# The norm's weights as one row, spread by a TensorE product, and the first tile scaled in halves

## The chip, the cores and the metric

The kernel runs on one core of a Trainium2 chip. The metric is the device time of one execution in microseconds (us); of the kernel before there are three timed runs and one profiled execution. TensorE is called PE, VectorE DVE, ScalarE ACT, GpSimd POOL, and SP is the engine that issues the DMAs.

## The reference

One decoder block on 1024 tokens of width 1024, float32. The part that matters here is the start:

```python
def rms_norm(x, g):
    xf = x.astype(jnp.float32)
    r = lax.rsqrt(jnp.mean(xf * xf, axis=-1, keepdims=True) + RMS_EPS)
    return (xf * r).astype(x.dtype) * g
...
        h = rms_norm(x, norm_g[layer])
        proj = h @ w_in[layer]
```

The projection is split into differential attention (q, k, v, z) and sparse attention (q, six kv parts, z, gates). Two of the kv parts are compressed: blocks of 32 tokens with a stride of 16 get a position term, go through a small two-layer network and give the compressed keys and values. Three sparse branches, the differential attention, two output gates, one output projection and the residual follow.

## The kernel before

Tokens are tiled by 128 (eight tiles). `load_x` brings one tile of x (512 KB) in, sums its squares on ACT (`xs`, `xss`), takes the power -0.5 on POOL (`xr`), multiplies by it and by the norm's weights on DVE (L235), transposes the tile on PE in two halves of four blocks (L152), and writes the transposed halves twice: rounded on ACT (`xh`, L240) and the remainder on DVE (`xl`, L241). The norm's weights lie in `ng_b`, 128 partitions times 1024, loaded by one DMA that reads the 4 KB row 128 times (L228).

`load_w` brings 512 or fewer columns of the projection in as eight tiles `raw` of 128 rows, splits each into a rounded part `whi` (ACT, L199) and a remainder `wlo` (POOL, L200); `raw` has four buffers. `mm_tokens` sums 24 products per token tile, three for each of eight k: whi by xh, wlo by xh, whi by xl (L208 to L210), in PSUM buffers that alternate between the kinds A and S.

The projection runs in chunks. The first (kv, 384 columns, `w_c0`) goes along with `load_x`; for each tile it copies the first two kv parts out (`kvraw`), transposes them, copies them (`kvt`, L263) and writes them to DRAM (`kv_d`, L264), and normalises a key head pair by `rms_heads`: square on ACT, sums `ss` on DVE, `r` on POOL (L135), the product `qn` on DVE (L143), a transpose on PE, then `kh` on ACT and `kl` on DVE. The second chunk (408 columns, `w_c1`) does the same with another key, and gates. The third (512 columns, nq) holds the compression: `cmp_flat` loads `kv_d` back as `kvT` (L317; one buffer, two loads per pass), adds the position term (`flat`, L320, DVE) and feeds the products at L332. There are eight `flat` steps.

The program's order on each engine isn't the order of the code: a scheduler builds it from its own timeline, and each engine then runs its list in order. SP issues all loads and stores on one queue; it has eight DMA semaphores that it uses in turn, so the ninth issue waits for the first to land.

Of the kernel before, what the change touches and what calls it, by code (L numbers as in the profile page):

```python
# [8 lines left out]
F32 = mybir.dt.float32  # L9
F32R = mybir.dt.float32r  # L10
AF = mybir.ActivationFunctionType
ALU = mybir.AluOpType
# [15 lines left out]
def block_kernel(ctx: ExitStack, tc: tile.TileContext, x, norm_g, w_in, dq_g, dk_g, lq1, lk1, lq2, lk2,  # L28
                 sub_g, nq_g, nk_g, cmp_pos, cmp_w1, cmp_b1, cmp_w2, w_out, out):
    nc = tc.nc  # L30
# [12 lines left out]
    def bcast(src, n):  # L43
        return bass.AP(tensor=src.tensor, offset=src.offset, ap=[[0, 128], [1, n]])

    def S_tile():
        return psS.tile([128, 1024], F32, tag="S", name="S")

    def T_tile():
        return psT.tile([128, 512], F32, tag="T", name="Tp")  # L50
# [97 lines left out]
    def transposed(src, nb):  # L148

        Tp = T_tile()  # L150
        for b in range(nb):
            nc.tensor.transpose(Tp[:, 128 * b:128 * b + 128], src[:, 128 * b:128 * b + 128], ident)  # L152
        return Tp[:, :nb * 128].rearrange("p (b t) -> p b t", t=128)
# [10 lines left out]
    with ExitStack() as p1:  # L164
# [16 lines left out]
        def load_w(wk, c0, c1, extra=None, perm=False, between={}):  # L181
            n = c1 - c0
            hi = wk.tile([128, 8, 512], F32R, tag="whi", name="whi")
            lo = wk.tile([128, 8, 512], F32R, tag="wlo", name="wlo")
            for k in range(8):
                for tt in between.get(k, ()):
                    load_x(between["xp"], tt)
                raw = wr.tile([128, 512], F32, tag="raw", name="raw")
                nc.sync.dma_start(raw[:, :n], w_in[128 * k:128 * k + 128, c0:c1])
                m = n  # L190
                if extra is not None:
                    m = n + extra[1] - extra[0]
                    nc.sync.dma_start(raw[:, n:m], w_in[128 * k:128 * k + 128, extra[0]:extra[1]])
                h_, l_, r_ = hi[:, k, :m], lo[:, k, :m], raw[:, :m]
                if perm:
                    h_ = h_.rearrange("p (g k d) -> p k g d", g=4, k=2)
                    l_ = l_.rearrange("p (g k d) -> p k g d", g=4, k=2)
                    r_ = r_.rearrange("p (k g d) -> p k g d", g=4, k=2)
                nc.scalar.activation(h_, r_, AF.Copy)  # L199
                nc.gpsimd.tensor_tensor(l_, r_, h_.bitcast(F32), op=ALU.subtract)  # L200
            return hi, lo
# [22 lines left out]
        def load_x(xp, tt):  # L224
            xt = xp.tile([128, T], F32, tag="xt", name="xt", bufs=5)
            nc.sync.dma_start(xt, x[128 * tt:128 * tt + 128])
            if tt == 0:
                nc.sync.dma_start(ng_b, bcast(norm_g, 1024))  # L228
            xs = xp.tile([128, T], F32, tag="xs", name="xs", bufs=1)
            ss = small.tile([128, 1], F32, tag="xss", name="xss")  # L230
            nc.scalar.activation(xs, xt, AF.Square, accum_out=ss)
            nc.vector.tensor_scalar(ss, ss, 1.0 / T, EPS, op0=ALU.mult, op1=ALU.add)
            r = small.tile([128, 1], F32, tag="xr", name="xr")
            nc.gpsimd.tensor_tensor(r, ss, neghalf[:, :1], op=ALU.pow)
            nc.vector.scalar_tensor_tensor(xt, xt, r, ng_b, op0=ALU.mult, op1=ALU.mult)  # L235
            t0 = 128 * tt
            for hf in range(2):
                X3 = transposed(xt[:, 512 * hf:512 * hf + 512], 4)
                k = slice(4 * hf, 4 * hf + 4)
                nc.scalar.activation(xh[:, k, t0:t0 + 128], X3, AF.Copy)  # L240
                nc.vector.tensor_tensor(xl[:, k, t0:t0 + 128], X3, xh[:, k, t0:t0 + 128].bitcast(F32), op=ALU.subtract)  # L241


        with ExitStack() as pc:
            xp = pc.enter_context(tc.tile_pool(name="xp", bufs=1))
            ng_b = xp.tile([128, 1024], F32, name="ng_b")
            load_x(xp, 0)
            w_c0 = load_w(wB, C_NKV, C_NKV + 384, between={"xp": xp, 3: (1,), 5: (2,), 7: (3,)})
            load_gains(1, nk_g, 3)
            for tt in range(NT):  # L250
                if tt + 4 < NT:
                    load_x(xp, tt + 4)
                if tt == 6:
                    load_consts(xp)
                t0 = 128 * tt
                if tt == 3:
                    w_c1 = load_w(wA, C_NKV + 384, C_NKV + 768, extra=(C_NG, C_NG + 24))
                A = mm_tokens(*w_c0, tt, 384)
                raw = st.tile([128, 512], F32, tag="qn", name="kvraw", bufs=3)
                nc.scalar.activation(raw[:, :256], A[:, :256], AF.Copy)  # L260
                kn = rms_heads(st, A[:, 256:384], 2, None)
                kvt = st.tile([128, 4, 128], F32, tag="z", name="kvt")[:, :2]
                nc.vector.tensor_copy(kvt, transposed(raw, 2))  # L263
                nc.sync.dma_start(kv_d[:, :, t0:t0 + 128].rearrange("b p t -> p b t"), kvt)  # L264
                k_pairs(kn, 1, G_KS, "nk", 0, tt)
# [435 lines left out]
    with ExitStack() as p3:  # L701
# [31 lines left out]
        for i, qt in enumerate(order):  # L733
# [7 lines left out]
            for h in range(4):  # L741
# [8 lines left out]
                                               op0=ALU.mult, op1=ALU.add)  # L750
# [17 lines left out]
            r = small.tile([128, 4], F32, tag="orr", name="orr")  # L768
# [30 lines left out]
```

## Time and profile before

| | us |
|---|---|
| three timed runs | 825.58, 829.02, 829.96 |
| median | 829.02 |
| profiled execution | 827.36 |
| its span, first to last instruction | 825.6 |
| PE busy | 777.7 (94%) |
| DVE, ACT, POOL busy | 515.8, 367.7, 358.5 |

The span is what the trace covers; the rest of the execution's time lies around it. PE's busy time counts pipelined products that overlap, so the distance from one product's start to the next says more than a product's own duration. A wait in brackets is the idle time of the engine before the instruction, with what ended it.

### The profile page before, as it was taken

Reading aid. Unit: us, or ns where it says so; the run is one execution under the profiler, and the core shown is the slowest. Engines: PE = TensorE matmul, PEld = TensorE weight load, DVE = VectorE, ACT = ScalarE, POOL = GpSimd, SP = SyncE. Lnnn points to the kernel's source line nnn. Section 1 sums busy time; section 2 is a strip of 40 time slices with the busy share of each in tenths; the row PEclk is TensorE's granted clock in tenths of the full one; section 3 lists DMA queues with packets and bytes.
Section 4 is the critical chain, followed back from the end, with each engine's and each line's share of the span. In section 5 each row is a group of like instructions: output and inputs, shape, how many; then the busy total and the mean of one; then the engine's idle time right before and its main releaser. Section 6 shows DMA issues by size and latency. Waiting matters only on the chain.

```text
span 825.6 us, 12841 instructions
## 1 busy us (share of the span) xinstructions
PE 777.7 (94%) x4457; PEld 643.0 (78%) x4457; DVE 515.8 (62%) x1183; ACT 367.7 (45%) x811; POOL 358.5 (43%) x385
## 2 busy tenths in 40 slices
PE   5999799999999999999899999999999798888997
PEld 4899788888888888888677788777777478687975
DVE  4654644368634338941698688785954296599843
ACT  6543131141323322121688656756564365477510
POOL 6834272250624525040487535354443135647421
PEclk9999899999999999999999999999999899999999
DMA  8637464151434423157643223130204504424133
GB/s 285 174 72 234 109 204 131 26 147 58 136 92 120 125 52 102 52 148 197 180 127 90 90 90 91 40 93 24 64 26 153 129 1 166 136 70 115 64 128 115
DMA packets 74257, 91.99 MB, mean 111 GB/s; under 512 B 13904, under 2 KB 48848, under 8 KB 74064
## 3 DMA queue, kind: packets, MB, share of 16 engines
q1 hardware_dynamic: 74192, 91.18, 38.3%
q8 instruction: 35, 0.57, 0.3%
q14 instruction: 30, 0.25, 0.1%
HBM read 63.89 MB, written 27.26 MB: 110 GB/s over the span
## 4 chain that ended last, share of the span: by engine, by line
PE 70%; DVE 11%; DMA 8%; POOL 4%; issue 3%; ACT 2%; SPq 2%; POOLq 0%; DVEq 0%; ACTq 0%
PE S L440 9%; PE A L632 6%; PE Tp L627 6%; PE S L210 5%; PE S L208 5%; PE S L209 5%; PE A L208 5%; PE A L210 5%; PE A L209 5%; PE A L480 3%; PE A L482 3%; PE A L481 3%; DVE P L444 2%; DMA raw<-in_w_in_dram 2%; PE Tp L152 2%
## 5 line engine op out<-in xcount | busy, mean ns | idle before, releaser
L446 ACT ACTIVATE P<-P,nm 128x128 f32<-128x128 f32 (+7 forms) x136 | 101.3, 749 | 35.8 <-DVE nm L444 26.3
L135 POOL TENSOR_TENSOR r<-ss,neghalf 128x8 f32<-128x8 f32 (+2 forms) x41 | 55.8, 1362 | 119.1 <-DVE ss L133 113.7
L200 POOL TENSOR_TENSOR wlo<-raw,whi 128x512 fp32r<-128x512 f32 (+2 forms) x64 | 82.5, 1314 | 51.4 <-ACT whi L199 51.4
L500 ACT ACTIVATE pT<-Tp 128x512 f32<-128x512 f32 (+3 forms) x118 | 66.2, 574 | 79.8 <-PE Tp L627 60.7
L208 PE MATMUL S<-whi,xh 128*128 128x512 f32 (+2 forms) x224 | 86.9, 388 | 1.2 <-ACT xh L240 0.7
L210 PE MATMUL S<-whi,xl 128*128 128x512 f32 (+2 forms) x224 | 87.1, 389 | 0.0
L208 PE MATMUL A<-whi,xh 128*128 128x512 f32 (+2 forms) x224 | 86.6, 387 | 0.0
L209 PE MATMUL S<-wlo,xh 128*128 128x512 f32 (+2 forms) x224 | 86.5, 386 | 0.0
L210 PE MATMUL A<-whi,xl 128*128 128x512 f32 (+2 forms) x224 | 86.0, 384 | 0.0
L209 PE MATMUL A<-wlo,xh 128*128 128x512 f32 (+2 forms) x224 | 85.9, 384 | 0.0
L596 POOL TENSOR_SCALAR P<-P,ssum 128x128 f32<-128x128 f32 (+7 forms) x72 | 52.9, 753 | 51.1 <-DVE ssum L592 31.8
L632 PE MATMUL A<-pT,vsw 128*64 128x256 f32 x528 | 67.3, 394 | 7.3 <-ACT pT L500 5.3
L440 PE MATMUL S<-nsaK,QH 128*128 128x384 f32 (+2 forms) x192 | 67.5, 360 | 2.0 <-DVE nm L444 1.8
L444 DVE CUSTOM_DVE_ANT_0 P<-S,D 128x128 f32<-128x128 f32 (+7 forms) x96 | 60.1, 660 | 14.5 <-PE S L440 8.3
L440 PE MATMUL S<-nsaK,QL 128*128 128x384 f32 (+2 forms) x192 | 60.7, 330 | 0.0
L632 PEld LDWEIGHTS A<-pT,vsw 128*64 128x64 f32 x528 | 35.2, 139 | 32.3 <-ACT pT L500 8.0
L596 POOL TENSOR_SCALAR Pw<-Pw,ssum 128x640 f32<-128x640 f32 (+3 forms) x56 | 40.7, 745 | 44.9 <-DVE ssum L592 37.5
L498 DVE COPY pT<-Tp 128x512 f32<-128x512 f32 (+3 forms) x62 | 38.5, 621 | 33.8 <-PE Tp L627 31.5
L415 POOL TENSOR_TENSOR QL<-q,QH 128x1024 fp32r<-128x1024 f32 x16 | 38.9, 2429 | 47.6 <-ACT QH L414 45.9
L160 DVE RECIPROCAL e<-e 128x512 f32<-128x512 f32 (+1 forms) x18 | 57.1, 3175 | 0.6
L199 ACT ACTIVATE whi<-raw 128x512 fp32r<-128x512 f32 (+2 forms) x64 | 36.5, 605 | 43.4 <-DMA raw<-in_w_in_dram 37.3
L480 PE MATMUL A<-woh,ch 128*128 128x512 f32 x128 | 51.9, 405 | 2.9 <-ACT ch L726 2.9
(186 smaller groups left out, 1820.5 us busy)
## 6 DMA issues: line engine op xcount, KB each, us to landing
raw<-in_w_in_dram SPq DMA_DIRECT2D x48, 256.0 KB, 3.1
xt<-in_x_dram SPq DMA_DIRECT2D x16, 512.0 KB, 3.8
w<-in_cmp_w_dram SPq DMA_DIRECT2D x16, 256.0 KB, 3.8
q<-nq_d SPq DMA_DIRECT2D x16, 256.0 KB, 4.2
xa_d<-xt SPq DMA_DIRECT2D x16, 256.0 KB, 2.0
q<-dq_d SPq DMA_DIRECT2D x16, 256.0 KB, 4.2
xt<-xa_d SPq DMA_DIRECT2D x8, 512.0 KB, 3.2
out_dram<-xt SPq DMA_DIRECT2D x16, 256.0 KB, 2.1
```

Of the source, the lines that this page charges most:

```text
L160: nc.vector.reciprocal(e, e)
L200: nc.gpsimd.tensor_tensor(l_, r_, h_.bitcast(F32), op=ALU.subtract)
L208: nc.tensor.matmul(A[:, :n], a, hi[:, k, :n], start=(k == 0), stop=False)
L209: nc.tensor.matmul(A[:, :n], a, lo[:, k, :n], start=False, stop=False)
L210: nc.tensor.matmul(A[:, :n], b, hi[:, k, :n], start=False, stop=(k == 7))
L440: nc.tensor.matmul(S[a][:, c0:c1], Q[:, heads[a]], Ks[a][:, w0 + c0 - o:w0 + c1 - o], start=Q is QH, stop=Q is QL)
L444: nc.vector.tensor_tensor_reduce(out=Ps[a][:, :n], in0=S[a][:, o:o + n], in1=biases[a], scale=-slopes[a], scalar=3e38, op0=ALU.add, op1=AL ...
L446: nc.scalar.activation(Ps[a][:, :n], Ps[a][:, :n], AF.Exp, scale=-1.0, bias=nm, accum_out=ssums[a])
L480: nc.tensor.matmul(A, ch[:, k], woh[:, k, c], start=(k == 0), stop=False)
L500: nc.scalar.activation(pT[:, :n], Tp[:, :n], AF.Copy)
L596: nc.gpsimd.tensor_scalar(P[:, :n], P[:, :n], ssum[:, g2, j:j + 1], 1.0, op0=ALU.mult, op1=ALU.mult)
L632: nc.tensor.matmul(O[64 * j:64 * j + 64, 256 * gp:256 * gp + 256], vsw[:, br, k0 + kt, 64 * j:64 * j + 64], pT[:, 256 * j:256 * j + 256], ...
```

## The change

The norm's weights are loaded as one row of 1024 on one partition. DVE fills a row of 128 ones. PE multiplies the ones by the row, half by half (fp32, one row deep), so each of the 128 output partitions gets the row; DVE copies both halves from PSUM to `ng_b`. For tile 0 only, the scaling at L235 is two instructions of 512 columns, each ahead of its half's transposes.

```diff
             if tt == 0:
-                nc.sync.dma_start(ng_b, bcast(norm_g, 1024))
+
+                g_row = xp.tile([1, 1024], F32, name="g_row")
+                nc.sync.dma_start(g_row, bass.AP(tensor=norm_g.tensor, offset=norm_g.offset, ap=[[1024, 1], [1, 1024]]))
+                ones = xp.tile([1, 128], F32, name="ones")
+                nc.vector.memset(ones, 1.0)
+                G = S_tile()
+                for hf in range(2):
+                    c = slice(512 * hf, 512 * hf + 512)
+                    nc.tensor.matmul(G[:, c], ones, g_row[:, c], start=True, stop=True)
+                    nc.vector.tensor_copy(ng_b[:, c], G[:, c])
...
-            nc.vector.scalar_tensor_tensor(xt, xt, r, ng_b, op0=ALU.mult, op1=ALU.mult)
             t0 = 128 * tt
+            if tt:
+                nc.vector.scalar_tensor_tensor(xt, xt, r, ng_b, op0=ALU.mult, op1=ALU.mult)
             for hf in range(2):
+                if tt == 0:
+                    c = slice(512 * hf, 512 * hf + 512)
+                    nc.vector.scalar_tensor_tensor(xt[:, c], xt[:, c], r, ng_b[:, c], op0=ALU.mult, op1=ALU.mult)
                 X3 = transposed(xt[:, 512 * hf:512 * hf + 512], 4)
```

The scheduler makes another order of the first part of the program from this. Lines behind the change have numbers 13 higher in the changed kernel. On DVE at the start of the program, before:

```order
L232 TENSOR_SCALAR xss<-xss 128x1
L235 SCALAR_TENSOR_TENSOR xt<-xt,xr,ng_b 128x1024
L241 TENSOR_TENSOR xl<-Tp,xh 128x4x128
L232 TENSOR_SCALAR xss<-xss 128x1
L235 SCALAR_TENSOR_TENSOR xt<-xt,xr,ng_b 128x1024
```

And the same place in the changed program:

```order
L241 TENSOR_SCALAR xss<-xss 128x1
L237 COPY ng_b<-S 128x512
L250 SCALAR_TENSOR_TENSOR xt<-xt,xr,ng_b 128x512
L241 TENSOR_SCALAR xss<-xss 128x1
L237 COPY ng_b<-S 128x512
L250 SCALAR_TENSOR_TENSOR xt<-xt,xr,ng_b 128x512
L246 SCALAR_TENSOR_TENSOR xt<-xt,xr,ng_b 128x1024
L241 TENSOR_SCALAR xss<-xss 128x1
L254 TENSOR_TENSOR xl<-Tp,xh 128x4x128
```

The sum of tile 1 now stands between the halves of tile 0, and the scaling of tile 1 ahead of the first `xl`. On ACT the squares of tiles 1 and 2 have moved ahead of the first `xh` in the same way.

On POOL, between the first chunk of the projection and the second, one piece of the difference (`wlo` 128x512 are the remainders of the nq weights, `r` the norms of one kv tile each):

```order
 L200 TENSOR_TENSOR wlo<-raw,whi 128x512 x4
 L135 TENSOR_TENSOR r<-ss,neghalf 128x2
+L200 TENSOR_TENSOR wlo<-raw,whi 128x512
+L135 TENSOR_TENSOR r<-ss,neghalf 128x2
 L200 TENSOR_TENSOR wlo<-raw,whi 128x512 x3
-L135 TENSOR_TENSOR r<-ss,neghalf 128x2
-L200 TENSOR_TENSOR wlo<-raw,whi 128x512
-L135 TENSOR_TENSOR r<-ss,neghalf 128x2 x7
+L135 TENSOR_TENSOR r<-ss,neghalf 128x2 x8
```

The last `r` of the first chunk stood behind seven of the eight `wlo`; it now stands behind all eight.

On DVE in the second chunk, where the `flat` steps stand, the first two of them before:

```order
L132 TENSOR_REDUCE ss<-qn 128x2
L320 TENSOR_TENSOR flat<-kvT,pos_sb 64x16x63
L133 TENSOR_SCALAR ss<-ss 128x2
L320 TENSOR_TENSOR flat<-kvT,pos_sb 64x16x63
L219 SCALAR_TENSOR_TENSOR kl<-Tp,gains,kh 128x128
L143 TENSOR_TENSOR qn<-A,r 128x128
```

And now:

```order
L333 TENSOR_TENSOR flat<-kvT,pos_sb 64x16x63
L143 TENSOR_TENSOR qn<-S,r 128x128
L219 SCALAR_TENSOR_TENSOR kl<-Tp,gains,kh 128x128
L289 TENSOR_SCALAR gates<-gates 128x24
L132 TENSOR_REDUCE ss<-qn 128x2
L333 TENSOR_TENSOR flat<-kvT,pos_sb 64x16x63
```

A `qn`, a `kl` and a gates step now stand between the two. At the end of the row of flats, the seventh and eighth, which had four small steps between them, now follow each other.

## Rows read from the trace of the kernel before

**Rows 1.** The page: busy tenths of PE in 40 equal slices of the span.

```profile
PE   5999799999999999999899999999999798888997
```

**Rows 2.** Stretches: from:to, length, busy us (instructions) by engine, clock, DMA share, GB/s.

```profile
0.00:17.35 17.35, 7.82 (x35) 6.41 (x35) 7.70 (x13) 11.54 (x21) 9.59 (x60) 1.00 0.90 306
17.35:36.00 18.65, 16.97 (x105) 16.17 (x104) 13.02 (x21) 11.41 (x26) 17.10 (x16) 1.00 0.59 159
36.00:70.00 34.00, 34.00 (x209) 33.43 (x208) 14.55 (x42) 13.91 (x36) 14.06 (x15) 1.00 0.54 140
70.00:112.00 42.00, 36.11 (x178) 32.88 (x177) 26.29 (x59) 10.51 (x47) 16.21 (x14) 0.92 0.55 142
112.00:640.00 528.00, 521.19 (x2938) 419.16 (x2939) 331.13 (x775) 229.39 (x486) 224.81 (x220) 1.00 0.36 102
```

**Rows 3.** Timeline, 0 to 18 us: start, duration, engine, line, operation [idle before].

```profile
1.23 0.42 SPq L228 DMA_DIRECT2D ng_b<-in_norm_g_dram  x1
...
4.25 1.06 ACT L231 ACTIVATE xs<-xt 128x1024 f32<-128x1024 f32 x1 [2.18 <-DMA xt<-in_x_dram]
...
6.65 1.28 DVE L235 SCALAR_TENSOR_TENSOR xt<-xt,xr,ng_b 128x1024 f32<-128x1024 f32 x1 [1.07 <-DMA ng_b<-in_norm_g_dram]
7.09 1.61 ACT L199 ACTIVATE whi<-raw 128x384 fp32r<-128x384 f32 x3 [1.69 <-DMA raw<-in_w_in_dram]
...
9.78 0.69 DVE L241 TENSOR_TENSOR xl<-Tp,xh 128x512 fp32r<-128x512 f32 x1 [1.84 <-ACT xh L240]
...
17.09 2.84 POOL L200 TENSOR_TENSOR wlo<-raw,whi 128x384 fp32r<-128x384 f32 x2 [1.61 <-ACT whi L199]
```

**Rows 4.** A DMA issue of the first 30 us: count, KB each, us to landing.

```profile
gains<-in_nsa_k_norm_g_dram SPq DMA_DIRECT2D x2, 0.8 KB, 6.0
```

**Rows 5.** Products on PE early and later; groups: count | busy us, mean ns.

```profile
11.33 0.52 PE L209 MATMUL A<-wlo,xh 128*128 128x384 f32 x1
11.65 0.52 PE L210 MATMUL A<-whi,xl 128*128 128x384 f32 x1
...
17.78 0.34 PE L209 MATMUL S<-wlo,xh 128*128 128x384 f32 x1
17.96 0.34 PE L210 MATMUL S<-whi,xl 128*128 128x384 f32 x1
...
L678 PE MATMUL A<-pcT,vcbd 128*128 128x512 f32 x16 | 8.3, 600 | 0.0
...
L498 DVE COPY pT<-Tp 128x512 f32<-128x512 f32 x48 | 32.9, 686 | 31.5 <-PE Tp L627 31.5
```

**Rows 6.** Timelines of POOL and DVE, and the chain's transfer, 66 to 82 us.

```profile
66.98 1.29 POOL L200 TENSOR_TENSOR wlo<-raw,whi 128x512 fp32r<-128x512 f32 x1 [3.04 <-ACT whi L199]
68.43 2.54 POOL L200 TENSOR_TENSOR wlo<-raw,whi 128x512 fp32r<-128x512 f32 x2 [0.15 <-ACT whi L199]
70.93 0.70 POOL L135 TENSOR_TENSOR r<-ss,neghalf 128x2 f32<-128x2 f32 x1
...
71.66 0.29 DVE L143 TENSOR_TENSOR qn<-S,r 128x128 f32<-128x128 f32 x1 [1.91 <-POOL r L135]
71.87 0.41 DVE L263 COPY kvt<-Tp 128x256 f32<-128x256 f32 x1
...
72.31 3.96 DMA kv_d<-kvt
...
79.80 1.91 DVE L320 TENSOR_TENSOR flat<-kvT,pos_sb 64x1008 f32<-64x1008 f32 x1 [0.56 <-DMA kvT<-kv_d]
```

**Rows 7.** Group of the flats, then timelines of DVE and PE, 105 to 109 us.

```profile
L320 DVE TENSOR_TENSOR flat<-kvT,pos_sb 64x1008 f32<-64x1008 f32 x8 | 15.2, 1900 | 6.1 <-DMA kvT<-kv_d 5.9
...
105.32 1.95 DVE L320 TENSOR_TENSOR flat<-kvT,pos_sb 64x1008 f32<-64x1008 f32 x1
...
107.83 0.29 DVE L143 TENSOR_TENSOR qn<-A,r 128x128 f32<-128x128 f32 x1 [0.17 <-POOL r L135]
...
108.29 0.27 PE L152 MATMUL Tp<-ident,qn 128*128 128x128 f32 x1
```

## The prediction

> **What bounds the kernel now.** I read the page's busy shares first. TensorE (PE) is busy for 94% of the span and, slice by slice, nearly everywhere except the first slice, a dip before 112 us and the last quarter [rows 1]. Then I cut the span where the order of instructions is cut: comparing the order of the two programs engine by engine, everything behind the first tile of the nq projection (before: about 112 us) stands as it stood, apart from tile numbers. So the change can act in four stretches [rows 2]: 0 to 17.35 us, where PE is idle for 9.5 us; 17.35 to 36, idle 1.7; 36 to 70, never idle; 70 to 112, idle 5.9. Behind 112 us PE is idle for 7 of 528 us, so what is gained or lost before is carried to the end nearly whole. Third came the start in time order [rows 3], with the DMA times [rows 4]; last the turn of the second weak stretch: what releases kv_d, the compression inputs that go through DRAM, and what they release [rows 6, 7].
>
> Two chains are to be seen. At the start one DMA queue feeds everything: tile 0 of x is there at 4.25, its scaling waits for the 512 KB copy of the norm's weights until 6.65, and the projection's weights stand behind that copy [rows 3, 4]. From 70 us on PE is held by VectorE (DVE), which in its own order waits four times for a pair of kvT loads between the steps that PE wants (the qn multiplications whose transposes stand between PE's products).
>
> **The change part by part.** The sum is made against the profiled execution, 827.36 us with a span of 825.6; the median of the three runs is 829.02.
>
> *Removed: 512 KB from the queue.* From 4.25 to 6.65, 2.4 us, the queue carried this copy [rows 3]. All loads behind it can land that much earlier. This is the most the start can give: -2.4.
>
> *Added: a 4 KB row, two products, two copies.* No row shows a one-partition load. It stands right behind tile 0, so 4.3 is my value for its landing; the late end is the 0.8 KB gains load of the same queue, 6.0 us from issue [rows 4], which from 1.23 gives 7.2. The Trainium skill (DMA: Bandwidth & Descriptors, Anatomy of one DMA) puts a transfer's fixed cost at about 2.0 us, a fit to transfers issued from GpSimd; by it the row would land at about 3.7, an estimate. The gains row does not agree with that: in this queue a small load takes what stands before it. By the page the sum below would come out 0.6 us lower.
>
> A 128x512 fp32 product is two records; the sixteen at line 678 are 8 products in 8.3 us, 1.04 each [rows 5]. At the start the products follow each other by 0.32 us, where later ones of that shape do by 0.18 [rows 5], so I take twice, 2.1 each: first half at 6.4, second at 8.5. A PSUM copy of 128x512 is 0.69 [rows 5], a half scaling 0.64, half of the 1.28 of tile 0 [rows 3].
>
> *Moved: the start.* In the new order DVE has, behind the first half's scaling, the sum of tile 1, and only then the second copy; ScalarE (ACT) has the squares of tiles 1 and 2 ahead of the first half of xh. Worked out: copy 6.4 to 7.1, half scaled 7.75; ACT, done with three weight tiles (1.61, [rows 3]) at 7.0, squares tile 1 (1.06 and its read-out) until 8.5; second copy and half until 9.95; tile 1 scaled until 11.2, and only then xl of tile 0, at 9.78 before: +1.4. That is the other end for the start. Against it, the fifth weight tile is issued earlier, ahead of the fifth x tile, and its low part, which PE waited for at 17.09 [rows 3], is ready at about 13.6. I get PE running without gaps from about 16.5 with 20 products done, against 17.35 with 14: 0.85 + 6 x 0.18 = 1.9 ahead. Of that some 1.0 is lost again before 36 us: in the new ACT order the second half of tile 2 stands behind a weight tile of the next matrix that must still land, and the stop for the last x tile behind GpSimd's (POOL) weight work stays. **Start: -0.9**, between -2.4 and +1.4. The products' buffer is one of two of its kind and is free again after the second copy, at 9.3; its next user comes later, at no cost. The cover of the rest is PE, solid from 36 to 70 [rows 2].
>
> *Moved: kv_d's last write.* POOL did, from 66.98, three low parts (1.29 and 2.54), then at 70.93 the r of the last kv tile; DVE waited for it 1.91 us, multiplied at 71.66 and copied kvt at 71.87, and kv_d was issued at 72.31 [rows 6]. The new order is one low part, the r of the tile before (0.70), three low parts, then this r. So 1.29 + 0.70 + 3 x 1.28 = 5.8 instead of 3.95 after 66.98: **+1.9**. Queued behind it on DVE are that qn and kvt, on SP the kvT loads, and on PE two transposes: the new PE order asks for the tile's kvraw transpose 12 products sooner, which now gains nothing and only makes PE wait for the POOL. Were the POOL's work early enough not to matter, those 12 products (0.18 each) would be a gain: ends -2.2 and +1.9.
>
> *Moved: the flats.* kv_d takes 3.96 us to land, kvT is loaded behind it, the first flat starts at 79.80, and the eighth ends at 107.27 [rows 6, 7]; its qn at 107.83 is the one that PE transposes at 108.29, so PE and this chain arrive together. Each flat is 1.90 [rows 7]. New: a qn, a kl, a gates step and a sum stand between flats 1 and 2, where one small step stood (+0.65, an estimate from steps like qn's 0.29 and kvt's 0.41 in [rows 6], which overlap a little), two small steps between 3 and 4, where none stood (+0.4), flats 7 and 8 follow each other where four stood (-0.6), but the root of the next qn now comes behind flat 8 instead of under it: small steps 0.3 and a POOL step of 0.70 with its handovers, where 0.56 was, about +0.75. **+1.2**, from 0 to +2.7; the upper end adds 1.5: PE's granted clock is 0.92 over this stretch [rows 2], so 0.08 x 42 = 3.4 us went to spells at the lower of its two levels (1.2 and 2.4 GHz) that followed stops of PE, and one spell more would be about half of that.
>
> **Sum**: -0.9 + 1.9 + 1.2 = +2.2, or 829.6 by the profiled execution's own time. Beside the median of before, 829.02, it would be 831.2. I write 830.
>
> **The rivals.**
> *The lead is kept* (chance 0.25). If the low parts run as early as their loads land, POOL is through before the last r is asked for, kv_d goes out on PE's word, and the start's whole 2.4 stays: 825.0; with the 12 products too, 822.8. For it: POOL is idle for 3.0 us before 66.98, waiting for loads [rows 6]. Against it: that wait is for SP's queue and follows PE.
>
> *The row lands late* (0.20), the slower side. If the 4 KB row takes the 6.0 us of the gains load, the products end at 9.3 and 11.4, and the second half is scaled at 11.4 + 0.7 + 0.65 = 12.75 instead of 9.95, tile 1 and xl of tile 0 behind it: +2.8 on the start. With the other terms -0.9 + 2.8 + 1.9 + 1.2 = +5.0, 832.4. It takes the kernel past 0.5% once the row lands 1.9 us late, at about 6.2.
>
> *It moves nothing* (0.15): the copy was never the limit, since ACT and the weight path pace the first tiles, and the two later terms are swallowed by PE's own late arrival. 827.4.
>
> **How the numbers follow.** The forecast has 0.40. This kernel's runs before spread from 825.58 to 829.96, so about 0.5% (4.1 us) is what a measurement can tell from no change; that the forecast and the idle case lie inside it, and the first rival mostly, makes "same" the likeliest: 0.62. Slower is most of the late row and the upper tail of the forecast, 0.22; faster the lower tail of the first rival, 0.16. The range takes the first rival's 825.0 less a us and the late row plus the half-rate spell and the offset of the median: 824 to 835.
>
> **What would show it.** Right: the first scaled half near 7.8 us, xl of tile 0 after 11; PE without gaps from 16 to 17; a stop of about 2 us in 24 to 28; POOL's r of the last kv tile right behind four low parts; first flat at or after 80; PE's transpose of that qn at 109.5 or later. Wrong: g_row landing after 6, or the first flat before 78. If the stretch behind 112 us took another time than the 714 us of before, the argument that it only carries the difference fails.

## The result: 1.4% slower, and the profile after

Four timed runs of the changed kernel have a median of 839.23 us (838.04 to 839.90), the kernel before beside them 828.01 (825.58 to 829.96): ratio 1.0142, 95% interval 1.0114 to 1.0170. The profiled execution took 839.56 us with a span of 837.9, 12.2 more than before (827.36). The forecast was 830, its range ended at 835.

The page's slices of PE and of its granted clock, which answer to [rows 1]:

```profile
PE   6897889999999999999999999999999699889997
...
PEclk9998999999999999999999999999999899999999
```

The weak slice is the fourth (63 to 84 us), where the kernel before has 9. The stretches, as in [rows 2] (from:to, length, busy us and instructions of PE, PEld, DVE, ACT, POOL, clock, DMA share, GB/s):

```profile
0.00:14.00 14.00, 7.65 (x18) 3.69 (x19) 7.10 (x14) 9.24 (x17) 10.22 (x59) 1.00 0.81 284
14.00:36.00 22.00, 19.55 (x110) 18.35 (x108) 16.04 (x22) 13.50 (x30) 19.18 (x18) 1.00 0.65 192
36.00:66.00 30.00, 27.78 (x157) 25.83 (x158) 12.46 (x33) 8.98 (x22) 4.86 (x6) 0.94 0.29 56
66.00:80.00 14.00, 7.96 (x38) 7.49 (x37) 4.95 (x12) 4.92 (x13) 10.87 (x11) 0.76 0.72 217
80.00:122.00 42.00, 37.29 (x189) 34.78 (x189) 25.68 (x59) 10.85 (x45) 7.50 (x11) 0.96 0.47 125
122.00:650.00 528.00, 522.26 (x2937) 420.53 (x2937) 330.43 (x775) 228.27 (x484) 226.21 (x221) 1.00 0.36 102
650.00:838.00 188.00, 164.41 (x1020) 137.27 (x1018) 119.83 (x276) 92.15 (x202) 76.86 (x64) 0.97 0.35 104
```

Before, PE was never idle from 36 to 70 us. Now it is idle for 2.2 us from 36 to 66 and for 6.0 from 66 to 80, and it runs parts of both at the lower clock. Behind, hardly anything has changed: from the first compression product to the end of the span it is 825.6 - 110.27 = 715.3 us before, 837.9 - 122.07 = 715.8 now. So nearly all of the 12 us arise ahead of 122 us.

In what follows, high parts are the rounded `whi` and `xh`, low parts the remainders `wlo` and `xl`. The start, SP, PE and DVE (start, duration, engine, line, operation, [idle before <- what ended it]), beside [rows 3]:

```profile
1.23 0.32 SPq L230 DMA_DIRECT2D g_row<-in_norm_g_dram  x1
...
3.94 2.04 PE L236 MATMUL S<-g_row,ones 1*128 1x512 f32 x2 [3.94 <-DMA g_row<-in_norm_g_dram]
6.77 2.07 PE L236 MATMUL S<-g_row,ones 1*128 1x512 f32 x2 [0.78 <-DVE ng_b L237]
...
6.02 0.69 DVE L237 COPY ng_b<-S 128x512 f32<-128x512 f32 x1 [0.52 <-PE S L236]
6.82 0.92 DVE L250 SCALAR_TENSOR_TENSOR xt<-xt,xr,ng_b 128x512 f32<-128x512 f32 x1
...
9.85 0.75 DVE L250 SCALAR_TENSOR_TENSOR xt<-xt,xr,ng_b 128x512 f32<-128x512 f32 x1
10.52 2.02 DVE L246 SCALAR_TENSOR_TENSOR xt<-xt,xr,ng_b 128x1024 f32<-128x1024 f32 x1
...
12.53 0.68 DVE L254 TENSOR_TENSOR xl<-Tp,xh 128x512 fp32r<-128x512 f32 x1
```

PE can start on the row 2.7 us after its issue, and the first scaled half ends at 7.74. But the second product waits for the copy of the first half, both lying in one PSUM tile, and the first low part `xl` comes at 12.53 instead of 9.78: VectorE scales tile 1 ahead of it, beside POOL's remainders in 2.02 us. The 24th product of the first chunk ends at 20.4 (before 19.4).

The middle of the first chunk, SP, DVE and PE:

```profile
27.48 0.37 SPq L226 DMA_DIRECT2D xt<-in_x_dram  x1
...
34.56 1.85 DVE L246 SCALAR_TENSOR_TENSOR xt<-xt,xr,ng_b 128x1024 f32<-128x1024 f32 x1
36.34 1.27 DVE L254 TENSOR_TENSOR xl<-Tp,xh 128x512 fp32r<-128x512 f32 x2
...
37.07 0.71 PE L152 MATMUL Tp<-ident,xt 128*128 128x128 f32 x4 [1.51 <-DVE xl L254]
```

The load of x tile 7 is issued at 27.48 (before 21.78), since SP's list now has it behind six of the eight loads of the second chunk's weights. VectorE's list has this tile's scaling ahead of two low parts of earlier tiles. It comes to the scaling only at 34.56, since the tile's square on ACT waited for the load until 32.29 and its sum and root followed; PE, which needs those low parts, stops. The 96th product ends at 41.0 instead of 36.6.

The tail of the first chunk, PE at the head of tile 7:

```profile
57.96 1.04 PE L152 MATMUL Tp<-ident,xt 128*128 128x128 f32 x8
59.25 0.45 PE L208 MATMUL S<-whi,xh 128*128 128x384 f32 x1 [0.25 <-ACT xh L253]
```

All eight transposes stand directly ahead of the tile's own products, so PE waits for the halves to be written. Tiles 5 to 7 take 18.9 us, before 16.1. The chunk ends at 64.5 instead of 57.5. Then comes the stop; ACT, SP, POOL, DVE and PE:

```profile
64.55 2.20 ACT L199 ACTIVATE whi<-raw 128x512 fp32r<-128x512 f32 x4 [1.18 <-PE S L210]
...
67.77 0.41 SPq L189 DMA_DIRECT2D raw<-in_w_in_dram  x1
...
73.16 0.63 ACT L199 ACTIVATE whi<-raw 128x512 fp32r<-128x512 f32 x1 [5.29 <-DMA raw<-in_w_in_dram]
73.69 0.26 ACT L130 ACTIVATE qn<-A 128x128 f32<-128x128 f32 x1
...
70.21 0.69 POOL L135 TENSOR_TENSOR r<-ss,neghalf 128x2 f32<-128x2 f32 x1
...
73.99 0.29 DVE L132 TENSOR_REDUCE ss<-qn 128x2 f32<-128x128 f32 x1 [4.64 <-ACT qn L130]
...
75.07 0.28 DVE L143 TENSOR_TENSOR qn<-S,r 128x128 f32<-128x128 f32 x1
...
69.10 0.35 PE L210 MATMUL A<-whi,xl 128*128 128x408 f32 x1
75.49 0.45 PE L152 MATMUL Tp<-ident,qn 128*128 128x128 f32 x1 [6.04 <-ACT whi L199]
```

The same high parts before, ACT:

```profile
57.55 2.19 ACT L199 ACTIVATE whi<-raw 128x512 fp32r<-128x512 f32 x4 [1.24 <-PE S L210]
...
66.27 0.63 ACT L199 ACTIVATE whi<-raw 128x512 fp32r<-128x512 f32 x1 [5.27 <-DMA raw<-in_w_in_dram]
```

Read the rows of the stop from the bottom. PE has 24 products of the second chunk behind the first chunk's end (69.10 is the last), then its list asks for a transpose of `qn`, 6.04 us of idle time. The root `r` for that `qn` was ready at 70.9. But VectorE's list has the sums of the *next* `qn` ahead of its multiplication (73.99, then 75.07); those sums need a square on ACT (73.69), which stands behind the high part of the fifth nq weight tile (73.16), which waits for that tile's load, issued at 67.77 behind the buffer that the first high and low parts set free. Only the start of this chain follows PE: the first four high parts wait for the chunk's last product, since `whi` is one buffer. The first high part to the fifth takes 8.6 us here and 8.7 before (57.55 to 66.27). Before, PE had work through all of it: its list asked for the same transposes 11 to 13 products later, and ACT's list had one more square ahead of the first high parts. After the stop the next products follow each other by 0.34 us instead of 0.185, at the lower clock (0.76 over 66 to 80 us).

### The profile page after: what moved, and what is told of

It reads as the page before. It is cut to its first block, busy times and chain, and to the rows that moved or that the text cites. A ratio compares the mean times of both kernels' runs of the same rounds, so it can differ in the third digit from the quotient of the medians.

```text
span 837.9 us, 12857 instructions
## 1 busy us (share of the span) xinstructions
PE 786.9 (94%) x4461; PEld 647.9 (77%) x4461; DVE 516.5 (62%) x1187; ACT 367.9 (44%) x811; POOL 355.7 (42%) x385
## 4 chain that ended last, share of the span: by engine, by line
PE 69%; DVE 10%; DMA 7%; issue 5%; POOL 4%; ACT 2%; SPq 2%; POOLq 0%; DVEq 0%; ACTq 0%
PE S L453 9%; PE A L645 6%; PE Tp L640 6%; PE S L210 5%; PE S L208 5%; PE S L209 5%; PE A L210 5%; PE A L208 5%; PE A L209 4%; PE A L495 3%; PE A L493 3%; PE A L494 3%; DVE P L457 2%; PE Tp L152 2%; DMA q<-dq_d 2%
## 5 line engine op out<-in xcount | busy, mean ns | idle before, releaser
L135 POOL TENSOR_TENSOR r<-ss,neghalf 128x8 f32<-128x8 f32 (+2 forms) x41 | 51.0, 1243 | 134.5 <-DVE ss L133 134.1
```

## The experiments

Each builds on the kernel before or after. The rules for the order use `tc.issue_after(x.ins)`, which puts what an engine is given in the block behind `x` in that engine's list. The edit asks for nothing else, but the scheduler makes the lists of all engines anew from it, so a rule can move other instructions too (e2, e9, e14). Rule P holds products 16 to 24 of a tile behind the next tile's first transposes, L the loads of the second chunk's weights behind x tile 7, Q the high parts of the nq weights behind the last k of the first chunk, V tile 1's scaling behind tile 0's first low part. The expectations call the first chunk c0 and the second c1; their letters stand for theories, which each names. "Chunk end" is the end of the 192nd product, "stop" PE's longest idle time from 62 to 80 us, "kv_d" the issue of its last write, all of the profiled execution; "ratio" is against the kernel before on the same chip.

| run | median us | ratio [95%] | chunk end | stop | kv_d | first flat |
|---|---|---|---|---|---|---|
| before | 828.0 | | 57.5 | 0.4 | 72.3 | 79.8 |
| after | 839.2 | 1.0142 [1.0114, 1.0170] | 64.5 | 6.0 | 82.8 | 88.5 |
| e1 halves only | 831.9 | 1.0059 [1.0037, 1.0082] | 58.8 | 5.1 | 77.3 | 82.8 |
| e2 after + rule P | 831.0 | 1.0039 [1.0017, 1.0061] | 60.3 | 0.3 | 75.5 | 83.5 |
| e3 after + rule L | 836.0 | 1.0098 [1.0070, 1.0126] | 61.4 | 5.4 | 80.5 | 86.0 |
| e4 row only | 838.3 | 1.0127 [1.0097, 1.0158] | 62.1 | 5.3 | 80.4 | 86.1 |
| e5 after + P + L | 830.0 | 1.0024 [1.0003, 1.0046] | 60.3 | 0.3 | 75.1 | 82.6 |
| e6 e5, two PSUM tiles | 830.7 | 1.0038 [1.0025, 1.0050] | 59.3 | 0.3 | 74.3 | 82.3 |
| e7 e1 + P + L | 827.7 | 0.9993 [0.9974, 1.0011] | 59.7 | 0.3 | 74.5 | 82.0 |
| e8 before, 7 x buffers | 833.1 | 1.0062 [1.0041, 1.0082] | 58.9 | 5.7 | 78.2 | 83.4 |
| e9 after + rule Q | 836.9 | 1.0107 [1.0078, 1.0136] | 64.5 | none | 78.9 | 84.4 |
| e10 before + Q | 830.2 | 1.0021 [1.0002, 1.0040] | 57.6 | none | 70.2 | 75.8 |
| e11 e7 + Q | 830.0 | 1.0029 [1.0007, 1.0051] | 59.6 | none | 72.2 | 77.8 |
| e12 e5 + Q | 832.4 | 1.0049 [1.0030, 1.0069] | 60.0 | none | 72.6 | 78.2 |
| e13 e8 + P | 828.7 | 1.0010 [0.9992, 1.0027] | 58.3 | 0.4 | 73.6 | 80.9 |
| e14 e5 + rule V | 835.0 | 1.0088 [1.0064, 1.0112] | 64.2 | 0.3 | 79.4 | 86.6 |
| e15 e6 + V | 829.7 | 1.0022 [1.0004, 1.0040] | 57.8 | 0.2 | 72.5 | 79.7 |

**e1, halves alone.** Against the kernel before:

```diff
+            if tt:
+                nc.vector.scalar_tensor_tensor(xt, xt, r, ng_b, op0=ALU.mult, op1=ALU.mult)
             for hf in range(2):
+                if tt == 0:
+                    c = slice(512 * hf, 512 * hf + 512)
+                    nc.vector.scalar_tensor_tensor(xt[:, c], xt[:, c], r, ng_b[:, c], op0=ALU.mult, op1=ALU.mult)
```

> Only the halving of tile 0's scaling; the norm's weights are still spread by the 512 KB load, so there is no row and no product on TensorE for it. Its lists begin as those of the kernel before, but from token tile 5 on TensorE's list is that of the changed kernel: both transposes of tiles 5, 6 and 7 stand directly ahead of the tile's own 24 products, and those of the last kv and k tiles at the head of the following products, where the kernel before has the next tile's first transposes 10 products ahead and the last k's at product 10 to 14. Theory P (the place of the transposes in TensorE's list costs the time): 835 to 841 us, first scaled kv write as late as in the changed kernel (81 to 84 us) and a stop of TensorE of 4 to 7 us at 68 to 77 us. Theory S (the row, its two products and copies at the start cost it): 825 to 830. Theory L (the loads of x tiles 6 and 7 stand behind loads of c1's weights): 827 to 832, since tile 7's load stands behind one such load only.

831.9 us: below P's range, above S's, at the upper end of L's. For P speaks the stop of 5.14 us, which it alone foretold, and that x tile 7 is loaded at 21.0 us here and not late. P's last kv write at 81 to 84 us was wrong too: it came at 77.3. The size is 4.5 us and not 8; with the old start the chunk's end comes only 1.4 later. So halving one scaling of 1.28 us moved the transposes of tiles 6 and 7 and of the kv and k tiles behind them to where the changed kernel has them.

**e2, rule P.**

```diff
-                nc.tensor.matmul(A[:, :n], a, hi[:, k, :n], start=(k == 0), stop=False)
...
+                with tc.issue_after(ahead.ins) if ahead and k >= 5 else nullcontext():
+                    nc.tensor.matmul(A[:, :n], a, hi[:, k, :n], start=(k == 0), stop=False)
...
-                A = mm_tokens(*w_c0, tt, 384)
+                A = mm_tokens(*w_c0, tt, 384, x_tp.get((tt + 1, 0)) if tt >= 4 else None)
```

> The changed kernel with one rule for the order and nothing else: from token tile 4 on, products 16 to 24 of a tile stand behind the next tile's first four transposes. Its start and SyncE's list are the changed kernel's; from token tile 5 on all five lists are word for word those of the kernel before. Theory P: 827 to 832 us, no stop of over 1 us between 62 and 80 us, last kv write 73 to 76 us. Theory S: 837 to 841. Theory L: 835 to 840, since tile 7's load is still issued at about 27.5 us.

831.0: 8.3 of the 11.2 us are gone, with row, products, halves and the start of all lists as in the changed kernel. The rule is written for PE, but from tile 5 on the scheduler gives all five engines the order of the kernel before, so these 8.3 us are the price of the whole order, not of PE's list alone. PE's timeline in tile 6 (the next tile's first half after the `qn`, the second after the last product), and the stretch of the stop:

```profile
52.64 0.27 PE L154 MATMUL Tp<-ident,qn 128*128 128x128 f32 x1
52.74 0.60 PE L154 MATMUL Tp<-ident,xt 128*128 128x128 f32 x4
...
54.95 0.60 PE L154 MATMUL Tp<-ident,xt 128*128 128x128 f32 x4
```

```profile
66.00:80.00 14.00, 13.60 (x77) 12.86 (x76) 3.66 (x13) 4.33 (x15) 7.26 (x8) 1.00 0.75 237
```

The chunk ends 4.1 us sooner, and from there to the first compression product it takes 53.0 us (changed kernel 57.6, before 52.8).

**e3, rule L.**

```diff
...
-                    w_c1 = load_w(wA, C_NKV + 384, C_NKV + 768, extra=(C_NG, C_NG + 24))
+                    with tc.issue_after(xt_ins[7].ins):
+                        w_c1 = load_w(wA, C_NKV + 384, C_NKV + 768, extra=(C_NG, C_NG + 24))
```

> The changed kernel with one rule: the loads of c1's weights stand behind the load of x tile 7. Tiles 6 and 7 are then loaded before any of them (changed kernel: tile 7 behind six of the eight). TensorE's list stays the changed kernel's in the tail of c0 and behind it. Theory P: 834 to 839 us with the 6 us stop before 80 us still there. Theory L: 827 to 832. Theory S: 837 to 841.

836.0, in P's range, and the stop stays. But the 96th product ends at 37.2 instead of 41.0, the chunk ends 3.0 sooner, and the time is 3.2 us less: the late load is a second, smaller cost.

**e4, row alone.** Against the changed kernel the halves go back to one scaling of tile 0.

> Only the row and its spreading by TensorE; tile 0 is scaled in one operation as in the kernel before. TensorE's list from token tile 5 on is the changed kernel's, and the load of x tile 7 stands behind seven of c1's eight. Theory P: 835 to 842 us. Theory L: 838 to 843, later than the changed kernel. A theory H, by which the halving of tile 0 brings the disorder and the row alone is harmless: 824 to 830.

838.3: the row alone brings the disorder too. H falls. It isn't later than the changed kernel, so L's part doesn't add up as written.

**e8, none of the change.** Only `name="xt", bufs=5` became `bufs=7`.

> The kernel before with seven buffers for x tiles instead of five and nothing of the change. Its loads of x come earlier (tile 7 ahead of the last two of c0's weights), and with that the scheduler puts the transposes of tiles 6 and 7 and those of the last kv and k tiles where the changed kernel has them. Theory P: slower than before by 2 to 6 us, 829.5 to 834, with a stop of 4 to 7 us at 66 to 77 us. If what costs time is an operation of the change: 825 to 828.5, as before or a little faster by the earlier loads.

```profile
69.50 0.45 PE L152 MATMUL Tp<-ident,qn 128*128 128x128 f32 x1 [5.66 <-ACT whi L199]
...
66.00:80.00 14.00, 10.51 (x50) 10.40 (x51) 5.20 (x16) 4.33 (x13) 7.05 (x7) 0.76 0.53 167
```

833.1 us, the same stop in the same place (PE's timeline and the stretch, clock 0.76), with no operation of the change in the program. **e13** is e8 with rule P:

> e8 (the kernel before with seven x buffers, nothing of the change) with the rule of e2, so that TensorE's list from token tile 6 on is that of the kernel before. Theory P: all of e8's loss goes, and its earlier x loads (96th product at 34.7 us against 36.6) stay as a gain: 825 to 828 us, no stop of over 1 us between 62 and 80. If e8 lost time by something else: 830 to 834.

828.7, just above P's 825 to 828, and the stop is gone. So P has three pairs, each without and with the rule: 1.0142 to 1.0039, 1.0059 to 0.9993 (e7, which has L as well), 1.0062 to 1.0010. The gain hoped for from the earlier loads didn't come: PE stops for 1.72 us at 37.28, and the chunk ends at 58.3.

**e5, P and L; e7, the same on the halves.**

> The changed kernel with both rules, that of e2 (products 16 to 24 behind the next tile's first transposes) and that of e3 (loads of c1's weights behind x tile 7). The sum of two theories, P with e2's measured part and L with e3's: c0's last product at 57 to 59 us (changed kernel 64.5, e2 60.3, e3 61.4), last kv write 72 to 74, no stop of over 1 us between 62 and 80; 826 to 829.5 us. If the two rules take away the same time and not two times, 830 to 832. A theory S by which the row and its products cost 3 us at the start by themselves: 830 to 832 with c0's last product at 60 or later.

> Only the halving of tile 0's scaling (e1, with the 512 KB load), with both rules. TensorE's list from token tile 5 on is that of the kernel before. Theory P: the 4.5 us of e1 go, 825.5 to 828.5 us, no stop of over 1 us between 62 and 80. If e1's time came from the halves at the start: 830 to 833.

830.0, with the chunk's end at 60.3 as in e2: the rules take away the same time, not two times, or S is right besides; the sum was wrong. e7 takes the time of the kernel before, within its interval. Its difference to e5, 2.4 us, would be what the row costs at the start with the tail in order; the two intervals just overlap, and in the traces the chunk's ends are only 0.6 us apart, so the size is not settled by this pair.

**e6, e14, e15: the start.** e6 gives the row's second product a PSUM tile of its own, rule V puts tile 1's scaling behind tile 0's first low part, e15 has both:

```diff
-                G = S_tile()
                 for hf in range(2):
+                    G = A_tile() if hf else S_tile()
...
+                with tc.issue_after(xl_ins[tt - 1, 0].ins) if tt == 1 else nullcontext():
+                    nc.vector.scalar_tensor_tensor(xt, xt, r, ng_b, op0=ALU.mult, op1=ALU.mult)
```

> As e5, and the row's second product goes into a PSUM tile of its own. In the changed kernel it stood at 6.76 us behind the copy of the first half; here it should start at 5.9 to 6.1, its copy end at 8.5 to 9, and the second half of tile 0 be scaled from 8.5 to 9 (changed kernel 9.85). If that wait sets the start, the 24th product comes 0.8 to 1.5 us ahead of e5's and the time is 825 to 828.5; if what sets it is VectorE's list behind it (tile 1's scaling ahead of the first low part), the 24th product stays within 0.4 us and the time that of e5.

> e5 (the changed kernel with the rules of e2 and e3) with one rule more: VectorE scales tile 1 behind tile 0's first low part, which in e5 and the changed kernel stood behind that scaling and ended at 13 us. If this place in VectorE's list is what the start costs: low part at 10.8 to 11.5, 24th product 1 to 2 us ahead of e5's 21.1, and 828 to 829.5 us against e5's 830.0. If it only moves the wait to tile 1's transposes: 48th product as in e5 (27.2) and 829.5 to 831.

> e14 with the row's two products in PSUM tiles of their own (as e6): second half of tile 0 scaled at 8.7 to 9.2 us instead of 9.85. If row, products and copies cost the start only by these two waits, the 48th product is at 24 to 25 as in the kernel before and the time 826 to 829; if the start stays behind because the copies and the divided scaling take VectorE 0.7 us each beside its other work, 48th product at 26 or later and 829.5 to 831.

e6 starts the product at 5.91 and the 24th product comes 0.9 sooner; yet the time is not less, which neither answer had. e14 is a miss on the wrong side, 835.0: in the list that came of rule V, VectorE stands for the load of a small vector with two low parts behind it (DVE, then PE):

```profile
23.95 0.29 DVE L114 TENSOR_TENSOR lprod<-lamv 128x128 f32<-128x128 f32 x1 [2.25 <-DMA lamv<-in_diff_lambda_k_dram]
24.16 1.28 DVE L261 TENSOR_TENSOR xl<-Tp,xh 128x512 fp32r<-128x512 f32 x2
...
24.89 1.12 PE L154 MATMUL Tp<-ident,xt 128*128 128x128 f32 x4 [3.67 <-DVE xl L261]
```

e15 doesn't meet that. VectorE in its start:

```profile
7.11 0.75 DVE L256 SCALAR_TENSOR_TENSOR xt<-xt,xr,ng_b 128x512 f32<-128x512 f32 x1
8.02 0.69 DVE L242 COPY ng_b<-A 128x512 f32<-128x512 f32 x1 [0.16 <-PE A L241]
...
9.27 0.95 DVE L256 SCALAR_TENSOR_TENSOR xt<-xt,xr,ng_b 128x512 f32<-128x512 f32 x1
10.15 0.68 DVE L261 TENSOR_TENSOR xl<-Tp,xh 128x512 fp32r<-128x512 f32 x1
```

The low part comes at 10.15, the chunk ends at 57.8 and the first flat starts at 79.7, as before. The 48th product, at 26.2, and the time of 829.7 were the second answer's. But with the two waits and the tail mended next to nothing of the row's cost is left at the chunk's end (0.3 us); either wait mended alone gained nothing. The 0.2% that remains isn't placed: in the trace of e15 the first compression product comes at 109.94 (before 110.27), PE's products stay within 0.5 us of those of the kernel before until 640 us, and the 1.9 us by which this execution is later arise behind, where the lists are those of before (clock 0.98 over 690 to 760 us, before 1.00). Over the traces without rule Q the part behind the first compression product takes 713.4 to 717.5 us, so one trace can't tell 2 us there.

**e9 to e12, rule Q** puts ACT's high parts of the nq weights behind the last k of the first chunk:

```diff
...
-        w_nq = load_w(wB, C_NQ, C_NQ + 512)
+        with tc.issue_after(kh_ins["nk", 0, 7].ins):
+            w_nq = load_w(wB, C_NQ, C_NQ + 512)
```

> The changed kernel with one rule on ScalarE: the rounding of nq's weights (high parts of L199 for the next chunk) stands behind the last k of c0 instead of between the last kv tiles. TensorE's list stays the changed kernel's up to the last c0 product (tiles 5 to 7 with both transposes directly ahead of their products). Theory Q (the stop at 69 to 75 us is ScalarE's and so VectorE's list held up by the high part that waits for raw tile 4 of nq): no stop of over 1.5 us between 66 and 80, last kv write 72 to 76 (changed kernel 82.8), 828 to 834 us. A theory R, by which the stop follows from TensorE's own list whatever ScalarE does, or by which the weights of nq come too late for their products: stop of 4 us or more, or one of that size moved to 85 to 112; 836 to 842.

> The kernel before with the rule of e9. TensorE's list stays that of before up to the last c0 products. Last kv write at 66 to 69 us instead of 72.3, first flat 73 to 76 instead of 79.8. By Q, with flats on the path, 822 to 827 us; if nq's weights are then what its first products wait for, 828 to 832.

> The halving alone (512 KB load) with all three rules: e7 with nq's high parts behind the last k. e7 took 827.7. By Q 822 to 826; if nq's weights come too late, 828 to 831.

> The changed kernel with all three rules: e5 with nq's high parts behind the last k. e5 took 830.0. By Q 824 to 828, and 1 to 3 us behind e11, which is what row and products cost at the start; if nq's weights come too late, 830 to 833.

In e9 the stop is gone. PE's list is the changed kernel's only up to the chunk's end: the transpose that the stop stood before is now asked for 11 products later, nearly where the kernel before has it. But its `qn` is ready at 66.81, ahead of the 24th product behind the chunk's end (69.17), after which the changed kernel asks for it. By these times PE would not have stopped for it in the old place either, so ACT's queue was the cause, as Q says. But the time is 836.9, in R's range: POOL now does the nq remainders beside the flats, and PE waits there (that `qn` on DVE, then POOL and PE):

```profile
66.52 0.29 DVE L143 TENSOR_TENSOR qn<-S,r 128x128 f32<-128x128 f32 x1 [0.88 <-POOL r L135]
...
82.56 6.60 POOL L200 TENSOR_TENSOR wlo<-raw,whi 128x512 fp32r<-128x512 f32 x4
...
89.78 2.67 POOL L200 TENSOR_TENSOR wlo<-raw,whi 128x512 fp32r<-128x512 f32 x1
...
93.06 0.30 PE L152 MATMUL Tp<-ident,qn 128*128 128x128 f32 x1 [1.47 <-DVE qn L143]
...
99.11 0.30 PE L152 MATMUL Tp<-ident,qn 128*128 128x128 f32 x1 [3.16 <-DVE qn L143]
```

Most remainders, 1.26 each in the changed kernel, take 1.65 to 2.67 here, and with two more stops behind these PE waits 9.8 us for `qn`. In e10 the first flat starts 4.0 us sooner than before, but the last ends at 114.2 instead of 107.3, and the time is 2 to 3 us worse; by the ratios e11 and e12 lose 0.36% and 0.25% (3.0 and 2.1 us) against e7 and e5. The gain expected by Q was wrong in all four, and all four times lie in the ranges of the other answer: the early start of the flats is lost where the weights' work falls among them. That answer named the nq products' wait for their weights; e9 shows PE waiting for `qn`.

## Why the prediction was wrong

- *Failed: "The cover of the rest is PE, solid from 36 to 70".* This step carried the forecast from the start to kv_d, and it was taken from the rows of the old order [rows 2]. In the new one the chunk's end is 7.0 us late: 1.0 at the 24th product, 3.4 more by the 96th (the late x load through ACT's and VectorE's lists, e3), 2.8 more in tiles 5 to 7 (the transposes at their head). Then PE idles for 6.0 more, behind ACT's queue. Rule P alone, which puts all lists from tile 5 on back, gives back 8.3 us; the two later terms of the sum are in that figure.
- *Failed with it: the transposes that the new order asks for "12 products sooner", priced at nothing or a gain.* What was compared was PE with POOL alone. The wait was for VectorE, behind ACT, behind a load; e8 shows the price without the change.
- *Mis-sized: kv_d's last write, +1.9.* It came 10.5 us later. The POOL work was right: four low parts and an r take 5.80 from 73.87, and 5.8 was worked out against [rows 6]. But it began 6.9 us later, and the last `kvt` waited for PE besides. POOL, SP, DVE and PE, with [rows 6, 7] to compare:

```profile
73.87 1.26 POOL L200 TENSOR_TENSOR wlo<-raw,whi 128x512 fp32r<-128x512 f32 x1 [2.96 <-ACT whi L199]
75.30 0.70 POOL L135 TENSOR_TENSOR r<-ss,neghalf 128x2 f32<-128x2 f32 x1 [0.17 <-DVE ss L133]
75.96 3.76 POOL L200 TENSOR_TENSOR wlo<-raw,whi 128x512 fp32r<-128x512 f32 x3
79.67 0.70 POOL L135 TENSOR_TENSOR r<-ss,neghalf 128x2 f32<-128x2 f32 x1
...
82.79 0.70 SPq L277 DMA_DIRECT2D kv_d<-kvt  x1
...
88.54 1.91 DVE L333 TENSOR_TENSOR flat<-kvT,pos_sb 64x1008 f32<-64x1008 f32 x1 [2.26 <-DMA kvT<-kv_d]
...
119.61 0.30 PE L152 MATMUL Tp<-ident,qn 128*128 128x128 f32 x1 [1.74 <-DVE qn L143]
```

- *The start, -0.9.* The 24th product ends 1.0 later, inside the ends given (-2.4 to +1.4), on the other side of the value. The landing (3.94 for 4.3) and the first scaled half (7.74 for 7.75) were right. The Trainium skill (DMA: Bandwidth & Descriptors, Anatomy of one DMA) has about 2.0 us as a transfer's fixed cost, a fit to transfers issued from GpSimd, and by it the estimate was 3.7. The row's 2.7 from issue to PE's start lies nearer to it than to the 6.0 of [rows 4]. Missed was the second product's wait for the first copy, and tile 1's scaling was taken at about 1.3 where it took 2.02 (the kernel before has 2.03 for it, at 11.64, a row that the prediction did not use): the rival of a late start was there with the wrong mechanism (the row's landing). "PE without gaps from 16 to 17" came true at 14.0, with products still at half pace until 17; the stop in 24 to 28 was 0.95 us at 28.9.
- *The flats, +1.2.* From the first flat's start to the last one's end 29.1 us, before 27.5: +1.7, inside 0 to +2.7. Whether its parts came as they were summed is not shown.
- *Right: the stretch behind only carries the difference.* 715.8 us against 715.3. ("Idle for 7 of 528 us" left out 640 to 825.6, where PE is idle for 24.0 us; it did no harm here.) The transpose of the last `qn`, "at 109.5 or later", came at 119.6.

None of the rivals had the tail's order as its mechanism, and the slower one ended at 832.4. By the prediction's own measure of 0.5%, "same" had 0.62 and "slower", which came, 0.22.

What stays open: why the scheduler, with any of four small edits (halves, row, both, two more buffers), falls into the same order of the tail (from tile 6 on) and with the kernel before didn't. The lists show that it does, not why. The residue of e15 against before, 0.2%, is hardly more than its interval tells from nothing, and its one trace doesn't tie it to the row.

## What to carry to other kernels

Where a scheduler makes the lists, an edit at the start can cost its time in the lists far behind it. So compare the lists as far as they differ, and for each engine that was solid, ask anew what its next instruction waits for through *all* the queues on the way, here PE, DVE, ACT and a load. And try the old order on the new program (one ordering rule gave back three quarters of the loss) before judging the change itself: the row cost 0.2 to 0.4%, if that, and the order 1%.

## What was not expected of the hardware

- VectorE's scaling of 128x1024, 1.28 us alone, took 2.02 beside POOL's remainders (10.52 in the start above); a half took 0.75 and, in e14, 1.56. The low parts, which read PSUM and one SBUF operand, took 0.67 to 0.69 throughout. The Trainium skill (SBUF — State Buffer, SBUF: two separate sides) has VectorE and GpSimd lock a shared port pair for a whole instruction when VectorE reads two SBUF inputs and GpSimd reads SBUF. The traces agree: the scaling reads two SBUF inputs, the remainders read SBUF, and the low parts, with one SBUF input, stay the same.
- Spreading the row took as long as the load that it replaced: two records of a product, 2.04 us, and a copy of 0.69 had the first half there at 6.71, the 512 KB load the whole at 6.65 [rows 3].
